# A planner's prices for GpSimd and wide matmuls, and a ring of five split weights instead of four, in a hybrid decoder trunk

## The chip, the cores and the metric

The kernel runs on one core of a Trainium2 chip. The metric is the device time of one execution in microseconds (us). TensorE is PE in the rows, its weight loads PEld, VectorE DVE, ScalarE ACT, GpSimd POOL, and SyncE, which issues the DMAs here, SP. Each engine works through its own instructions in order; semaphores hold an instruction until those of other engines are done.

## The reference

One layer of a decoder trunk for 2048 prompt tokens and 8 requests of 4 tokens with the same weights (width 1024, MLP width 4096), all in fp32:

```python
h = _rmsnorm(x, norm1_g) * (1.0 + sc1) + sh1
proj = h @ w_in                     # 1024 -> 2824 columns
z, xbc, dt, frw, us5 = jnp.split(proj, list(IN_SPLITS), axis=-1)
y_ssd, ... = _ssd_mixer(z, xbc, dt, ...)      # Mamba-2, chunked
y_rw, ...  = _rwkv_mixer(frw, ...)            # RWKV-7, a recurrence
y_s5, ...  = _s5_mixer(us5, ...)              # complex diagonal SSM + GLU
mix = jnp.concatenate([y_ssd, y_rw, y_s5], axis=-1) @ w_out
x = x + g1 * mix
h2 = _rmsnorm(x, norm2_g) * (1.0 + sc2) + sh2
ff = jnp.square(jax.nn.relu(h2 @ mlp_w1)) @ mlp_w2
x = x + g2 * ff
```

A last RMSNorm follows, and the mixers' new states are outputs too.

## The kernel before

**Tiles and stages.** The tokens are four blocks of 512 columns; block 1 also carries the 32 columns of the short requests (544, computed as two pieces of 272). Stage by stage, PE projects the four blocks through `w_in`, then for blocks 0 and 1 computes `w_out` and the MLP, and from about 2050 us on `paired` computes the rest for blocks 2 and 3 together, with fewer products by sums of blocks. The mixers of all blocks run between, as narrow fp32 matmuls and work of DVE, ACT and POOL, and fill in beside the wide matmuls.

**Wide matmuls and split weights.** A wide product is made of fp32r matmuls, 128 x 128 weights by 512 or 272 columns. For accuracy each operand is split into a high and a low part, and three matmuls (high x high, high x low, low x high) make one. A weight tile of 128 x 1024 comes by DMA into one of four raw buffers in `arena` and is used as two halves of 512 columns, 12 matmuls each for 512 columns of tokens. `wprep` has ACT cast a half's high part, and `wlow` has POOL subtract it from the raw half for the low part; both land in one of `NWH` = 4 slots of a ring in `arena_r`. `whalf` (for the projections and the MLP) and `wop` (in `paired`) take the next half and call `wprep` and `wlow` for later ones. `gemm2` starts a projection with two products at once and so holds four halves, all slots of the ring.

**Memory.** `arena_r` holds 14336 columns of split activations, then the ring. `arena_b` (14336) and the part of `arena` behind A_C (A_L columns) hold the mixers' temporaries; a mixer is admitted while the costs of those running are at most ROOM = 18364 columns. A generator that finds no room yields; an evacuation of a wide product (`mal`) waits.

**What sets the order.** The program is written out once, in the order in which instructions are called, with a clock for each engine in `Plan`: every call adds a price (`Eng.__getattr__`) and starts at the latest of its engine's clock and its operands' times. Between matmuls, `pump` steps the generators of the mixers whose operands are ready by PE's clock. So the prices decide behind which wide matmul a narrow one is written, and how far ahead of use a cast is written follows from `wprep` and `wlow`. All engine instructions are called at line 201, so the rows all show L201, and tiles have the names `arena`, `arena_b`, `arena_r`, `arena_t` (it takes the place of `arena_b` in `paired`) and `bk` for the eight PSUM banks.

Of the kernel before, what the change touches and what calls it, by code (L numbers as in the profile page):

```python
# [22 lines left out]
LS = 4  # L23
W = 544
A_T = 14336
A_R = A_T + 5600
NRB = 4
A_C = 7296 + 1024 * NRB
A_L = 11360
A_F = A_C + A_L  # L30
ROOM = 18364
NPLAIN = 2
# [159 lines left out]
class Eng:  # L192
# [3 lines left out]
    def __getattr__(self, op):  # L196
        fn = getattr(self.real, op)
        plan, name = self.plan, self.name

        def call(*a, **k):  # L200
            r = fn(*a, **k)  # L201
            aps = [x for x in list(a) + list(k.values()) if hasattr(x, "tensor")]
            out, ins = aps[:1], aps[1:]
            n = 1
            for c in out[0].shape[1:]:
                n *= c
            dma = 0
            if name == "PE":
                m = out[0].shape[0]
                if "r" in str(ins[0].dtype)[-1]:  # L210
                    cost = max(n / 2.4 + 2.5, 107)
                elif op == "transpose":
                    cost = 110
                elif m > 64:
                    cost = max(n / 0.6, 215)
                elif m > 32:
                    cost = max(n / 0.86, 100)
                else:
                    cost = max(n / 1.4, 68)
            elif name == "DVE":  # L220
                ps = any(x.tensor.name.startswith("bk") for x in aps)
                if op in ("tensor_scalar", "tensor_copy", "memset") and not ps:
                    cost = 65 + 0.53 * n
                elif op == "tensor_reduce":
                    i = 1
                    for c in ins[0].shape[1:]:
                        i *= c
                    cost = 70 + 1.04 * i
                elif op == "tensor_tensor_scan":
                    cost = 70 + 2.1 * n  # L230
                elif op == "reciprocal":
                    cost = 70 + 8.3 * n
                else:
                    cost = 72 + 1.04 * n + (30 if ps else 0)
            elif name == "ACT":
                cost = 95 + 0.833 * n
            elif name == "POOL":
                cost = 60 + (2.4 if op == "tensor_tensor" else 0.9) * n
            else:
                cost = 0  # L240
                dma = 4.0
                for c in out[0].shape:
                    dma *= c
            plan.run(name, cost, out, ins, dma)
            return r

        return call
# [3 lines left out]
def layer_kernel(ctx: ExitStack, tc: tile.TileContext, d, o, dbg=None):  # L251
# [7 lines left out]
    arena = sbp.tile([128, A_F], F32, name="arena")  # L259
    arena_r = sbp.tile([128, A_R], F32R, name="arena_r")  # L260
    swap = [ExitStack()]
# [4 lines left out]
    M = Mem(arena[:, 0:A_C], A_C)  # L266
    M1 = Mem(arena[:, A_C:], A_L)
    MB1 = Mem(arena_b, A_T)
    MT = Mem(arena_r[:, 0:A_T], A_T, True)
    MR = Mem(arena_r[:, A_T:], A_R - A_T, True)  # L270
    A1, AR, AT, AM = [MB1, M1], [MR], [MT], [M, MB1, M1]
# [405 lines left out]
            yield from finish()  # L677


    NWH = 4  # L680
    wring = [(MR.get(512), MR.get(512)) for _ in range(NWH)]
    wbuf = M.get(1024 * NRB)
    wraw = [wbuf.f[:, 1024 * i:1024 * i + 1024] for i in range(NRB)]
# [2 lines left out]
    class WS:  # L686
# [3 lines left out]
        pos = 0  # L690
# [9 lines left out]
    def whalves(i):  # L700
        hi, lo = wring[i % NWH]
        return hi, lo, wraw[i // 2 % NRB][:, 512 * (i % 2):512 * (i % 2) + 512]
# [3 lines left out]
    def wprep(upto):  # L706
        while WS.ready < min(upto, len(wops)):
            i = WS.ready
            wload(wops[i][0] + 1)
            hi, lo = wring[i % NWH]  # L710
            sm = wops[i][1]
            if sm is None:
                act(hi.r, whalves(i)[2])
            else:
                wsrc[i] = sm.get(wops[i][2])
                act(sm.shape(hi.r), wsrc[i])
            WS.ready += 1

    def wlow(upto):
        while WS.low < min(upto, WS.ready):  # L720
            i = WS.low
            hi, lo = wring[i % NWH]
            sm = wops[i][1]
# [18 lines left out]
    def whalf():  # L742
        i = WS.pos
        WS.pos += 1
        wprep(i + 3)
        wlow(i + 1)
        hi, lo = wring[i % NWH]
        return hi.r, lo.r

# [104 lines left out]
    def pieces(hasS):  # L854
        return [(0, 272), (272, 544)] if hasS else [(0, BT)]
# [16 lines left out]
    def gemm(xs, hasS, drop=()):  # L872
        nk = len(xs)
        got, ws = [], []
        for (c0, c1) in pieces(hasS):
            bk = gbank()
            assert bk is not None
            n = c1 - c0
            cnt = 0
            for k in range(nk):  # L880
                if k % 4 == 0 and k // 4 == len(ws):
                    ws.append(whalf())
                if k % 4 == 2:
                    wlow(WS.pos + 2)
                hi, lo = ws[k // 4]
                xh, xl = xs[k]
                h_, l_ = hi[:, 128 * (k % 4):128 * (k % 4) + 128], lo[:, 128 * (k % 4):128 * (k % 4) + 128]
                for i, (w_, x_) in enumerate(((h_, xh), (h_, xl), (l_, xh))):
                    x_ = x_[:, c0:c1]
                    t = plan.when([w_, x_], "PE")  # L890
                    while t > plan.clk["PE"] + 150 and pump(t - plan.clk["PE"]):
                        pass
                    mm(bk[:, 0:n], w_, x_, start=cnt == 0, stop=cnt == nk * 3 - 1)
                    cnt += 1
                    if i == 2 and drop and c1 >= BT:
                        free(*drop[k])
                    if cnt % SLOT == 0 and cnt < nk * 3:
                        pump()
            got.append((bk, c0, c1))
        return got  # L900

    def gemm2(acts, hasS):
        units = [(m, p) for m in range(2) for p in pieces(hasS)]
        nt = 2
        bks = [wait_for(gbank, "bank") for _ in units]
        cnt = 0
        for k in range(8):
            if k > 0 or not WS.pos:
                wait_for(lambda: len(acts) > k, "acts")
            if k == 0:  # L910
                pos = WS.pos
                wprep(pos + 2 * nt)
                wlow(pos + 2 * nt)
                WS.pos += 2 * nt
                wait_for(lambda: len(acts) > k, "acts")
            if k == 6:
                wprep(WS.pos + 1)
                wlow(WS.pos + 1)
            xh, xl = (x.r for x in acts[k])
            for u, (m, (c0, c1)) in enumerate(units):  # L920
                hi, lo = (w.r for w in wring[(pos + 2 * m + k // 4) % NWH])
                h_, l_ = hi[:, 128 * (k % 4):128 * (k % 4) + 128], lo[:, 128 * (k % 4):128 * (k % 4) + 128]
                for i, (w_, x_) in enumerate(((h_, xh), (h_, xl), (l_, xh))):
                    x_ = x_[:, c0:c1]
                    t = plan.when([w_, x_], "PE")
                    while t > plan.clk["PE"] + 150 and pump(t - plan.clk["PE"]):
                        pass
                    mm(bks[u][:, 0:c1 - c0], w_, x_, start=k + i == 0, stop=k == 7 and i == 2)
                    cnt += 1
                    if cnt % SLOT == 0 and cnt < 24 * len(units):  # L930
                        pump()
        wprep(WS.pos + 3)
        for m in range(2):
            yield [(bks[u], c0, c1) for u, (j, (c0, c1)) in enumerate(units) if j == m]

# [1674 lines left out]
    def wop():  # L2610
        i = WS.pos
        WS.pos += 1
        wprep(i + 3)
        wlow(i + 1)
        hi, lo = wring[i % NWH]
        return hi.r, lo.r

    def product(bk, w, col, units, first, k_done=0):
        n = len(units) * 3
        cnt = 0  # L2620
        for k, (xh, xl) in enumerate(units):
            c = col + 128 * k
            for w_, x_ in ((w[0], xh), (w[0], xl), (w[1], xh)):
                w_ = w_[:, c:c + 128]
                t = plan.when([w_, x_], "PE")
                while t > plan.clk["PE"] + 150 and pump(t - plan.clk["PE"]):
                    pass
                T.matmul(bk, w_, x_, start=first and cnt == 0, stop=cnt == n - 1, skip_group_check=True)
                cnt += 1
                if cnt % SLOT == 0 and cnt < n:  # L2630
                    pump()
                if cnt == n // 2:
                    wlow(WS.pos + 1)
        pump()

    def paired(last, ys):
# [555 lines left out]
```

## Time and profile before

| | us |
|---|---|
| median of 3 runs | 2949.0 (2939.87 to 2949.55) |
| the profiled execution | 2948.27 |
| its span, first to last instruction | 2946.5 |
| PE busy | 2709.7 (92%) |
| DVE busy | 1916.1 (65%) |
| POOL busy | 1474.9 (50%) |
| ACT busy | 1099.3 (37%) |
| mean granted clock of TensorE | 0.950 |

A row of windows gives busy time and the count of instructions for each engine in a stretch, and the granted clock (PEclk): 1.00 is 2.4 GHz, 0.50 is 1.2 GHz. A row of waits says which instructions stood idle for which releaser, the total, the number and the longest. A row of the timeline gives the start, the time, the engine, the operation, the tiles (written <- read), the shape and the count of merged instructions, and in brackets the idle time before it and what ended it. Times of matmuls overlap, so a step is read from a long run of equal ones.

### The profile page before, as it was taken

How to read it: one execution, taken by the hardware profiler on the slowest of the kernel's cores; microseconds unless marked ns; L12 is line 12 of the kernel's file. 1: busy time of each engine (PE TensorE's matmuls, PEld its weight loads, DVE VectorE, ACT ScalarE, POOL GpSimd, SP SyncE). 2: the span in 40 equal slices, each digit the busy share in tenths (PEclk: the TensorE clock that was granted, in tenths of full speed). 3: DMA queues.
4: the chain of work that ended last, by engine and by line, in shares of the span. 5: the costliest groups of instructions: out<-in, count | busy, mean ns of one | idle time of the engine just before them, and what ended most of it. 6: DMA issues, size and time to landing. Idle time of an engine off the chain costs nothing.

```text
span 2946.5 us, 44466 instructions
## 1 busy us (share of the span) xinstructions
PE 2709.7 (92%) x16267; PEld 2250.1 (76%) x16267; DVE 1916.1 (65%) x3553; ACT 1099.3 (37%) x2049; POOL 1474.9 (50%) x1274
## 2 busy tenths in 40 slices
PE   7888988999997999999898998999996999989997
PEld 5567876676776777777687898999985778868886
DVE  5885786676675535556776768563354644478777
ACT  5354343444332333433333432333444222344332
POOL 2255344344454434354432444343444877768883
PEclk9898999999998899999998999999998999999998
DMA  8466546545643333345542453422453344374431
GB/s 281 147 208 201 183 159 206 170 140 154 197 122 136 111 117 117 115 146 159 176 142 74 140 192 95 146 92 89 139 190 109 140 150 157 144 274 143 143 136 58
DMA packets 329766, 441.86 MB, mean 150 GB/s; under 512 B 87620, under 2 KB 199364, under 8 KB 329548
## 3 DMA queue, kind: packets, MB, share of 16 engines
q1 hardware_dynamic: 329548, 439.02, 44.7%
q8 instruction: 128, 2.10, 0.3%
q14 instruction: 90, 0.74, 0.1%
HBM read 331.77 MB, written 107.18 MB: 149 GB/s over the span
## 4 chain that ended last, share of the span: by engine, by line
PE 48%; DVE 9%; issue 3%; POOL 1%; DMA 1%; ACT 1%; SPq 0%; DVEq 0%; POOLq 0%; ACTq 0%
PE bk L201 48%; DVE arena_b L201 5%; DVE arena L201 3%; POOL arena_r L201 1%; DVE arena_r L201 1%; ACT arena_b L201 1%; DMA sphid<-arena 0%; DVE arena_t L201 0%; ACT arena_r L201 0%; POOL arena L201 0%; SPq L201 0%; DMA arena_r<-sphid 0%; ACT arena L201 0%; DMA arena_b<-sph 0%; DMA arena_b<-spk 0%
## 5 line engine op out<-in xcount | busy, mean ns | idle before, releaser
L201 PE MATMUL bk<-arena_r 128*128 128x512 f32 (+1 forms) x9376 | 1861.4, 353 | 121.7 <-ACT arena_r L201 51.3
L201 PEld LDWEIGHTS bk<-arena_r 128*128 128x128 f32 x9376 | 1509.1, 193 | 379.5 <-ACT arena_r L201 60.8
L201 POOL TENSOR_TENSOR arena_r<-arena,arena_r 128x512 fp32r<-128x512 f32 (+1 forms) x795 | 1084.8, 1379 | 1051.3 <-ACT arena_r L201 929.0
L201 ACT ACTIVATE arena_r<-arena 128x512 fp32r<-128x512 f32 x757 | 459.8, 626 | 452.0 <-PE bk L201 257.1
L201 ACT ACTIVATE arena_b<-bk 128x512 f32<-128x512 f32 (+10 forms) x478 | 202.1, 446 | 787.2 <-PE bk L201 542.6
L201 PE MATMUL bk<-arena_t,arena_r 128*128 128x512 f32 x1584 | 397.9, 401 | 26.1 <-DVE arena_t L201 12.4
L201 PEld LDWEIGHTS bk<-arena_t,arena_r 128*128 128x128 f32 x1584 | 301.8, 191 | 102.2 <-DVE arena_t L201 14.9
L201 DVE SCALAR_TENSOR_TENSOR arena<-bk,arena 128x512 f32<-128x512 f32 (+1 forms) x370 | 232.5, 641 | 213.0 <-PE bk L201 207.5
L201 DVE TENSOR_TENSOR arena_b<-arena_b 128x256 f32<-128x256 f32 (+19 forms) x481 | 262.3, 555 | 51.4 <-ACT arena_b L201 34.3
L201 POOL TENSOR_TENSOR arena<-arena 128x512 f32<-128x512 f32 (+1 forms) x142 | 208.4, 1467 | 87.3 <-DVE arena L201 81.2
L201 DVE TENSOR_TENSOR arena<-arena,bk 128x512 f32<-128x512 f32 (+2 forms) x189 | 124.6, 669 | 174.4 <-PE bk L201 143.1
L201 PE MATMUL bk<-arena_b 32*32 32x128 f32 (+11 forms) x2424 | 221.4, 273 | 6.2 <-DVE arena L201 3.4
L201 PEld LDWEIGHTS bk<-arena_b 32*32 32x32 f32 (+6 forms) x2424 | 183.4, 149 | 44.9 <-issue 17.7
L201 DVE SCALAR_TENSOR_TENSOR arena_b<-arena_b,arena 128x512 f32<-128x512 f32 (+4 forms) x234 | 141.5, 619 | 36.9 <-POOL arena_b L201 16.7
L201 PE MATMUL bk<-arena,arena_b 128*64 128x128 f32 (+8 forms) x1035 | 138.2, 279 | 25.5 <-DVE arena_b L201 18.7
L201 PE MATMUL bk<-arena 128*64 128x128 f32 (+7 forms) x1214 | 132.2, 322 | 30.9 <-DVE arena L201 16.5
L201 DVE TENSOR_TENSOR arena_r<-arena_b,arena_r 128x512 fp32r<-128x512 f32 (+1 forms) x113 | 90.5, 808 | 100.3 <-ACT arena_r L201 99.5
L201 DVE TENSOR_TENSOR arena<-arena 128x512 f32<-128x512 f32 (+14 forms) x188 | 144.7, 779 | 14.6 <-ACT arena L201 8.6
L201 PEld LDWEIGHTS bk<-arena,arena_b 128*128 128x128 f32 (+4 forms) x1035 | 111.2, 163 | 54.3 <-DVE arena_b L201 21.1
L201 PEld LDWEIGHTS bk<-arena 128*64 128x64 f32 (+4 forms) x1214 | 107.2, 166 | 58.4 <-DVE arena L201 17.6
L201 ACT ACTIVATE arena_b<-arena_b 128x512 f32<-128x512 f32 (+4 forms) x176 | 106.3, 610 | 119.9 <-DVE arena_b L201 99.4
L201 DVE TENSOR_TENSOR arena_b<-arena_b,arena 128x4 f32<-128x4 f32 (+13 forms) x223 | 118.3, 552 | 18.9 <-POOL arena L201 6.6
(79 smaller groups left out, 1664.5 us busy)
## 6 DMA issues: line engine op xcount, KB each, us to landing
arena<-in_w SPq DMA_DIRECT2D x196, 512.0 KB
arena<-in_w_in SPq DMA_DIRECT2D x88, 512.0 KB
sphid<-arena SPq DMA_DIRECT2D x112, 256.0 KB
arena<-in_ada_w SPq DMA_DIRECT2D x16, 1024.0 KB
arena<-in_w_out SPq DMA_DIRECT2D x32, 512.0 KB
arena_t<-sphid SPq DMA_DIRECT2D x30, 512.0 KB
arena_b<-spk SPq DMA_DIRECT2D x29, 512.0 KB
arena_r<-sphid SPq DMA_DIRECT2D x26, 512.0 KB
```

What stands on the lines that cost most here:

```text
L201: r = fn(*a, **k)
```

## The change

Two things. The prices of `Eng.__getattr__` change for fp32r matmuls on PE (from n/2.4 + 2.5 to n/2.36 + 9 ns) and for POOL: copies 150 + 1.1 n instead of 60 + 0.9 n, `tensor_tensor` up to 16 columns (these are powers, for reciprocal roots) 320 + 210 n, wider ones 70 + 2.45 n instead of 60 + 2.4 n. And the ring has five slots; `wprep` and `wlow` are called for one half more ahead at each place. The fifth slot's 1024 columns come out of A_L. The operations and their shapes are the same; with the prices, the order of all engines changes.

```diff
-A_R = A_T + 5600
+A_R = A_T + 6624
-A_L = 11360
+A_L = 10336
                 if "r" in str(ins[0].dtype)[-1]:
-                    cost = max(n / 2.4 + 2.5, 107)
+                    cost = max(n / 2.36 + 9, 107)
             elif name == "POOL":
-                cost = 60 + (2.4 if op == "tensor_tensor" else 0.9) * n
+                if op == "tensor_copy":
+                    cost = 150 + 1.1 * n
+                elif op == "tensor_tensor" and n <= 16:
+                    cost = 320 + 210 * n
+                elif op == "tensor_tensor":
+                    cost = 70 + 2.45 * n
+                else:
+                    cost = 60 + 0.9 * n
...
-    NWH = 4
+    NWH = 5
+    AHEAD = NWH - 3
...
     def whalf():
         i = WS.pos
         WS.pos += 1
-        wprep(i + 3)
-        wlow(i + 1)
+        wprep(i + AHEAD + 2)
+        wlow(i + AHEAD)
...
                 if k % 4 == 2:
-                    wlow(WS.pos + 2)
+                    wlow(WS.pos + AHEAD + 1)
...
                 pos = WS.pos
-                wprep(pos + 2 * nt)
+                wprep(pos + 2 * nt + AHEAD - 1)
                 wlow(pos + 2 * nt)
...
             if k == 6:
-                wprep(WS.pos + 1)
-                wlow(WS.pos + 1)
+                wprep(WS.pos + AHEAD)
+                wlow(WS.pos + AHEAD)
...
-        wprep(WS.pos + 3)
+        wprep(WS.pos + AHEAD + 2)
...
     def wop():
         i = WS.pos
         WS.pos += 1
-        wprep(i + 3)
-        wlow(i + 1)
+        wprep(i + AHEAD + 2)
+        wlow(i + AHEAD)
...
                 if cnt == n // 2:
-                    wlow(WS.pos + 1)
+                    wlow(WS.pos + AHEAD)
```

**ACT at the start of block 1's projection (its pair of products).** `arena_r<-arena 128x512` is the cast of a weight half, `arena_r<-arena_b 128x544` that of an activation of block 1, `arena_b<-bk_70 128x512 x2` the evacuation of block 0's last product, beside which the pair's first matmul is written. Before:

```order
L201 ACTIVATE arena_b<-arena_b,arena 128x512
L201 ACTIVATE arena_r<-arena 128x512
L201 ACTIVATE arena_r<-arena_b 128x544
L201 ACTIVATE arena_b<-arena_b,arena 128x512
L201 ACTIVATE arena_b<-bk_70 128x512 x2
L201 ACTIVATE arena_r<-arena_b 128x544
L201 ACTIVATE arena_r<-arena 128x512 x2
L201 ACTIVATE arena<-bk_76 128x256
```

Now:

```order
L201 ACTIVATE arena_r<-arena 128x512
L201 ACTIVATE arena_r<-arena_b 128x544
L201 ACTIVATE arena_b<-arena_b,arena 128x512
L201 ACTIVATE arena_r<-arena 128x512
L201 ACTIVATE arena_b<-bk_70 128x512 x2
L201 ACTIVATE arena_r<-arena_b 128x544
L201 ACTIVATE arena_b<-arena_b,arena 128x512
L201 ACTIVATE arena_r<-arena_b 128x544
L201 ACTIVATE arena_r<-arena 128x512 x2
L201 ACTIVATE arena_b<-bk_73,arena 128x512
```

The `x2` was the pair's third and fourth half, the third with no matmul left between its cast and its use; now the third is cast ahead of the evacuation, and the `x2` is the fourth and a fifth half, 41 matmuls ahead of the fourth's use.

**ACT later in the same projection, where block 2's input is first read.** `arena_b<-arena_b 128x512` are squares of block 2's `x`, just loaded, and the rows with `bk` around them evacuate products of block 1. Before:

```order
L201 ACTIVATE arena_b<-bk_70 128x8x4
L201 ACTIVATE arena_b<-bk_70,arena 128x32
L201 ACTIVATE arena_b<-arena_b 128x512 x2
L201 ACTIVATE arena_r<-arena 128x512
L201 ACTIVATE arena<-bk_73 128x272
```

Now:

```order
L201 ACTIVATE arena_b<-bk_76 128x8x4
L201 ACTIVATE arena_b<-bk_76,arena 128x32
L201 ACTIVATE arena_b<-arena_b 128x512
L201 ACTIVATE arena<-arena_b 128x512
L201 ACTIVATE arena_r<-arena 128x512
L201 ACTIVATE arena<-bk_70 128x272
```

Nothing moved: two squares (the second now writes to `arena`) still stand directly ahead of the cast of a half, which has 0 matmuls before its first use before and 5 now.

**POOL where the solve of block 0's recurrence begins.** `arena_r<-arena,arena_r 128x512` is the low part of a weight half, the memsets clear the solve's tile, and the copies are of the convolution's edge columns. Before:

```order
L201 COPY arena_b<-arena 128x3
L201 COPY arena<-arena_b 128x3
L201 MEMSET arena_b 64x1024
L201 MEMSET arena_b 64x32
L201 TENSOR_TENSOR arena_r<-arena,arena_r 128x512
L201 COPY arena_b<-arena 128x4 x2
```

Now:

```order
L201 COPY arena<-arena_b 128x24
L201 TENSOR_TENSOR arena_r<-arena,arena_r 128x512
L201 MEMSET arena_b 64x1024
L201 MEMSET arena_b 64x32
L201 TENSOR_TENSOR arena_r<-arena,arena_r 128x512 x2
L201 TENSOR_TENSOR arena<-arena_b,arena 128x1
```

A low part stands ahead of the memsets now, and the first one behind them is used 39 matmuls later instead of at once.

## Rows read from the trace of the kernel before

**Rows 1.** Windows, the first 2250 us: length, busy by engine (instructions), PEclk, DMA share, GB/s.

```profile
0.00:2250.00 2250.00, 2073.24 (x13575) 1738.85 (x13576) 1447.26 (x3015) 862.59 (x1685) 951.32 (x914) 0.95 0.47 152
```

**Rows 2.** Waits of PE in the first 2250 us: total us, times, longest.

```profile
PE bk L201 <- POOL arena_r L201: 41.8, 19, 9.0
PE bk L201 <- ACT arena_r L201: 37.3, 11, 9.5
PE bk L201 <- DVE arena L201: 24.4, 15, 10.6
PE bk L201 <- DVE arena_b L201: 23.2, 13, 13.4
...
PE bk L201 <- POOL arena L201: 6.2, 5, 1.9
```

**Rows 3.** Timeline of PE at its longest waits for `arena_r`.

```profile
222.71 0.82 PE L201 MATMUL bk<-arena_r 128*128 128x272 f32 x2 [7.28 <-ACT arena_r L201]
...
257.29 0.82 PE L201 MATMUL bk<-arena_r 128*128 128x272 f32 x2 [9.54 <-ACT arena_r L201]
...
420.99 1.27 PE L201 MATMUL bk<-arena_r 128*128 128x272 f32 x4 [8.73 <-POOL arena_r L201]
...
473.80 1.22 PE L201 MATMUL bk<-arena_r 128*128 128x512 f32 x2 [8.99 <-POOL arena_r L201]
...
683.29 0.80 PE L201 MATMUL bk<-arena_r 128*128 128x512 f32 x1 [4.03 <-ACT arena_r L201]
...
1471.10 1.27 PE L201 MATMUL bk<-arena_r 128*128 128x272 f32 x4 [5.42 <-POOL arena_r L201]
...
1598.54 0.82 PE L201 MATMUL bk<-arena_r 128*128 128x272 f32 x2 [5.66 <-ACT arena_r L201]
```

**Rows 4.** Timeline of ACT and POOL: what stood ahead of three late weights.

```profile
255.41 1.31 ACT L201 ACTIVATE arena_b<-arena_b 128x512 f32<-128x512 f32 x2 [11.73 <-DMA arena_b<-in_x]
...
418.29 1.15 POOL L201 MEMSET arena_b<- 64x1024 f32 x2 [7.98 <-DMA spl<-arena_b]
...
466.97 1.62 POOL L201 TENSOR_TENSOR arena_b<-arena_b 128x504 f32<-128x504 f32 x1 [5.94 <-DVE arena_b L201]
```

**Rows 5.** Windows, stretches at half clock behind late weights, and the sum of all 15.

```profile
195.10:198.50 3.40, 3.40 (x30) 2.16 (x32) 3.40 (x5) 3.40 (x7) 3.34 (x4) 0.50 0.68 263
219.00:229.20 10.20, 5.83 (x24) 5.51 (x25) 10.03 (x19) 2.49 (x6) 6.23 (x5) 0.50 0.46 154
249.70:263.30 13.60, 6.01 (x18) 4.26 (x19) 2.74 (x4) 5.45 (x13) 5.08 (x7) 0.50 0.85 299
...
416.90:427.20 10.30, 6.21 (x27) 6.21 (x28) 6.86 (x15) 0.69 (x2) 5.92 (x9) 0.50 0.69 194
...
468.10:478.40 10.30, 4.60 (x19) 4.41 (x20) 4.51 (x6) 1.26 (x2) 8.74 (x11) 0.50 0.77 213
...
1468.20:1475.10 6.90, 4.00 (x18) 4.00 (x19) 6.52 (x13) 3.13 (x6) 4.79 (x5) 0.51 0.93 308
1594.50:1604.80 10.30, 5.71 (x23) 5.39 (x24) 9.90 (x20) 6.54 (x11) 4.28 (x3) 0.50 0.15 51
...
sum 95.70, PE 66.26 PEld 57.49 DVE 63.36 ACT 27.25 POOL 59.92; mean PE 4.42 PEld 3.83 DVE 4.22 ACT 1.82 POOL 4.00
```

**Rows 6.** Timeline of PE, long runs of wide matmuls of both widths at 2.4 GHz.

```profile
2718.25 19.22 PE L201 MATMUL bk<-arena_r 128*128 128x512 f32 x84
...
2039.77 20.40 PE L201 MATMUL bk<-arena_r 128*128 128x272 f32 x161
```

**Rows 7.** Lines of POOL by form: count, busy us, mean ns, idle before.

```profile
L201 POOL TENSOR_TENSOR arena_r<-arena,arena_r 128x512 fp32r<-128x512 f32 x791 | 1082.4, 1383 | 1051.3 <-ACT arena_r L201 929.0 <-PE bk L201 69.6 <-ACT arena_b L201 22.7
...
L201 POOL TENSOR_TENSOR arena<-arena_b,arena 128x4 f32<-128x4 f32 x16 | 17.7, 1105 | 42.5 <-DVE arena_b L201 42.2
```

**Rows 8.** Timeline of PE, the longest wait behind 2250 us.

```profile
2267.54 0.79 PE L201 MATMUL bk<-arena_t,arena_r 128*128 128x512 f32 x1 [7.70 <-ACT arena_t L201]
```

**Rows 9.** Lines of DVE by form: additions with one input from PSUM, with both from SBUF.

```profile
L201 DVE TENSOR_TENSOR arena<-arena,bk 128x512 f32<-128x512 f32 x178 | 119.8, 683 | 173.4 <-PE bk L201 142.3 <-ACT arena_r L201 24.7 <-DMA arena<-in_w 4.1
L201 DVE TENSOR_TENSOR arena<-arena 128x512 f32<-128x512 f32 x112 | 112.6, 1017 | 12.4 <-ACT arena L201 8.5 <-POOL arena_t L201 1.5
```

## The prediction

> **What bounds the kernel now.** I read the windows first, for which engine is full and at what clock; then PE's waits; then the timeline at the longest of them; last, the queues that held the late operand. In the first 2250 us PE is busy for 2073.24, DVE for 1447.26, POOL for 951.32 and ACT for 862.59 [rows 1]: PE is the bound, so what counts is PE's idle time and the time that it spends at 1.2 GHz. Up to there only one tile holds both weights and activations, `arena_r`, and the waits on it come to 41.8 (from POOL, which makes the low parts) and 37.3 us (from ACT, which makes the high parts), 79.1 together in 30 waits [rows 2]. Almost all of it is split weights that came late. Seven of the 30 make 49.65 us [rows 3]; the other 23 make 29.5, 1.3 each.
>
> Why they are late is seen on the queue in front of the late operand. At 257.29 PE waits 9.54 us for a cast that stands on ACT behind two squares, and the first of these waited 11.73 us for a load of `x`. At 420.99 and 473.80 the low part stands on POOL behind a memset that waited 7.98 us for a store, and behind a subtraction that waited 5.94 us for DVE [rows 4]. These are queues in order: a wait of the mixers ahead of a split becomes a wait of PE when the split is needed soon after it.
>
> Each such wait costs twice. In 15 stretches (95.7 us), each at or just behind one of them, the granted clock is 0.50, the 1.2 GHz level, after PE had stood idle; PE is busy for 66.26 us in them [rows 5], work that takes half as long at 2.4 GHz: 33.1 us lost. So weights that come late cost 79 + 33 = 112 us of this execution, 3.8%.
>
> **The change part by part.** *Ring of five.* Casts and splits are neither added nor removed; each is written one half earlier. A half is 12 matmuls of 512 columns, at 19.22 us / 84 = 0.229 us, so 2.75 us; in block 1, whose columns go in two pieces of 272, it is 12 matmuls a piece at 20.40 / 161 = 0.127, so 1.5 us [rows 6]. That alone covers nearly all of the 23 short waits, but not the seven long ones, and the order says more than the mean: of 1440 casts and low parts, 45 stand fewer than 12 matmuls ahead of their first use before, and 14 now; the median goes from 35 matmuls to 48. Scaled by these counts, 79.1 x 14/45 = 24.6 us stay and **54.5 go**. The long waits taken one by one agree. At the three starts of a projection pair (7.28, 4.03 and 5.66 us) the third and fourth halves were cast at the pair's own start; now the third is cast before it and the fourth stands 41 matmuls ahead: gone. The wait of 9.54 stays: the order of ACT has the squares ahead of a needed cast as before. Behind the memset the low part now stands 39 matmuls ahead, 39 x 0.127 = 5.0 us, so 8.73 - 5.0 = 3.7 stay. That of 8.99 goes (3 matmuls before, over 30 now). Of 5.42 take off one half, 2.7 stay. That is 16 us, and of the short ones (14 - 3)/(45 - 7) of 29.5 = 8.5: 24.5 in all.
>
> *Clock.* The stretches at 249.70 and 1468.20 stay, that at 416.90 by half: 6.01 + 4.00 + 3.1 = 13 us of busy time; of the rest, 66.26 - 6.0 - 4.0 - 6.2 - 4.6 (that at 468.10) = 45.4, the same 11/38, 13 us. These 26 us at 1.2 GHz still lose 13: **20 of 33 go** [rows 5].
>
> *Given back.* While PE stood, the mixers' chains on DVE ran on. In 8 of the 15 stretches DVE is busy for over 95%, from the one at 195.10 to the one at 1594.50, 41 us together, though it is at 64% in the first 2250 us [rows 1, 5]. With PE no longer standing there, a part of this work becomes what PE waits for. None of it is the lower bound, all 41 us the upper; I take a third, **+14**, because in the other seven stretches DVE has room.
>
> *Prices of wide matmuls.* They go from 215.8 to 226 ns at 512 columns and from 115.8 to 124 at 272; the rows say 229 and 127 [rows 6], so the plan now runs at PE's pace. It also takes away a spare of 4.5%: a narrow matmul put 3 us behind its operand used to get 3.0 x 229/215.8 = 3.18 us and now gets 3.04. Over the 28 waits on DVE's results [rows 2] that is 0.14 x 28 = 4 us at most. The Trainium skill speaks against this price: "TensorE: Matmul & The Clock Gate", section "Wait — 56ns, not 53.3ns?", gives N/2.4 + 2.5 ns from start to start, 215.7 ns at 512 columns, which is the old formula. By it the new price would be too high, narrow matmuls would come too early, and the sum would be some 4 us longer; the trace's 229 ns disagrees with it, and the measurement decides.
>
> *Prices of GpSimd.* The power of a 128x4 tile was planned at 70 ns and takes 1105, now priced 1160; the 128x512 split was 1289, takes 1383 and is now 1324 [rows 7]. Consumers of powers are set a microsecond later. PE's waits on such results are 6.2 us [rows 2], so the gain is 0 to 6; I set it against the 4 us above: 0, with ends of -6 and +4.
>
> *Others, at nothing.* 1024 columns go from the mixers' memory to the ring (rival, below). A pair asks for a fifth cast at its start, 0.6 us on ACT, under PE's first 12 matmuls; uncovered, 0.6 us for each pair, some 5 us. On SP a fourth weight load stands ahead of block 1's first loads of `x`, which nothing waits for so early. From 2250 us on PE's waits are on activations, as the 7.70 us at 2267.54 [rows 8], in chains that the change leaves in place.
>
> **Sum.** The profiled execution took 2948.27 us (span 2946.5), 0.7 below the median of 2949.0, so the sum stands for either: 2948.3 - 54.5 - 20 + 14 = **2888**. Its own bounds: with nothing given back and all of the 112 us gone, 2948 - 112 - 6 = 2830; with all 41 given back, 2948.3 - 74.5 + 41 + 4 + 5 = 2924.
>
> **The rivals.** *DVE takes the place of the late weights.* For it: the 8 full stretches, and mixers that now run denser, with more splits beside DVE's work. A DVE addition with two inputs from SBUF takes 1017 ns where one with an input from PSUM takes 683 [rows 9]. If DVE's and POOL's meetings stretch the 41 us by that ratio, 61 us come back, and the gain is 74.5 - 61 = 13: 2935, within 0.5%. Against it: 64% is no full engine. The Trainium skill has a rule for this, "SBUF — State Buffer", section "Who interferes with whom": DVE instructions with two SBUF inputs and GpSimd's reads exclude each other for a whole instruction; the two means agree with it.
>
> *The shorter memory stalls PE: slower.* The mixers' temporaries have 24672 columns instead of 25696 while admission still counts 18364, so what is left for stores, squares and evacuations falls from 7332 to 6308. Where none is free, the evacuation of a wide product waits and the next one is written only after it. A spot of this kind costs what the stretch at 219.00 shows, 10.2 us with PE busy for 5.83 at half clock: 4.4 + 2.9 = 7.3 us [rows 5]. It decides from 8 to 9 spots on (60.5 / 7.3); 12 give 2888 + 88 = 2976. Against it: the 2,700th of the 2,812 narrow matmuls stands behind 6,716 wide ones before and 6,652 now, so the mixers aren't pushed back.
>
> *The casts are early but blocked all the same.* The slot that a cast waits for is freed at the same matmul as before, so if that were what held ACT and POOL, nothing would change: 2949. Against it: the rows name a load, a store and DVE as what held them [rows 4].
>
> **How the numbers follow.** Forecast (2860 to 2925): 0.66. Nearly all late weights gone (2830 to 2860): 0.06. DVE in their place, 0.12, half of it just over and half within 0.5%. Blocked all the same: 0.07. Memory, slower: 0.09. 0.5%, 15 us, is about what a measurement of this kernel tells from no change. Faster 0.66 + 0.06 + 0.06 = 0.78, within 0.13, slower 0.09. The range of 8 in 10 leaves out the slower case, the blocked one and the lowest: 2850 to 2936.
>
> **What would show it.** PE's waits on `arena_r` up to 2250 us should fall from 79 to some 25, from POOL and from ACT alike, with one of 7 to 10 us left where squares of `x` stand ahead of a cast. With 26 of 66 us of that work left, some 58 us less are spent at 1.2 GHz, and the mean clock of the first 2250 us should rise from 0.95 to 0.96. Waits on DVE's tiles may rise by 14 us. The last 700 us should be the same within a few us. I am wrong if the waits on `arena_r` stay above 50, if waits on DVE grow by more than 40, or if PE waits with narrow work missing where before it had none.

## The result and the profile after

The changed kernel takes **2910.4 us** (median of 4 runs, 2904.6 to 2913.6) where the kernel before takes 2948.6 beside it: a ratio of **0.9875 (95% interval 0.985 to 0.9899)**, 38 us less. The prediction was 2888, with a range of 2850 to 2936: right in direction and inside the range, but 22 us too good. Its profiled execution has a span of 2908.4 us, 38.1 less than before.

The first 2206 us of it hold about as many matmuls as the first 2250 before [rows 1], and end at the same place of the program. The windows of after, in the columns of [rows 1] (PE, PEld, DVE, ACT, POOL, granted clock, DMA share, GB/s), for that part and for the rest:

```profile
0.00:2206.00 2206.00, 2052.99 (x13567) 1726.03 (x13567) 1453.12 (x3014) 862.85 (x1684) 962.38 (x916) 0.96 0.48 155
2206.00:2908.00 702.00, 641.69 (x2700) 516.10 (x2700) 470.32 (x540) 236.01 (x366) 522.57 (x358) 0.95 0.40 143
```

And the rest of the kernel before:

```profile
2250.00:2946.00 696.00, 636.44 (x2694) 511.25 (x2692) 468.88 (x538) 236.68 (x364) 523.57 (x361) 0.95 0.40 144
```

So 44 us are won up to that place and 6 are lost behind it, in `paired`. PE's waits in the first 2206 us of after, to be held against [rows 2]:

```profile
PE bk L201 <- DVE arena_b L201: 50.8, 21, 13.7
PE bk L201 <- DVE arena L201: 19.9, 9, 7.1
PE bk L201 <- ACT arena L201: 17.6, 5, 5.9
PE bk L201 <- ACT arena_r L201: 16.2, 9, 8.0
...
PE bk L201 <- POOL arena_r L201: 4.6, 5, 1.5
```

The waits on `arena_r` from POOL and ACT fell from 79.1 to 20.8 us (some 25 were expected); those on DVE's `arena_b` rose from 23.2 to 50.8. One wait of 8.0 on ACT's `arena_r` is new, and it is not for a weight at all.

**An accounting that closes.** Of every trace I took three sums: PE's waits of over 60 ns; which of them are for a half of split weights (told by the address of the late operand), up to the first matmul of `paired`; and half of PE's busy time in the stretches at 1.2 GHz, since that work takes about half as long at 2.4 (in after, wide matmuls follow each other at 427 ns in the slow stretches and 230 in the others with 512 columns, at 227 and 125 with 272, so what is lost is 45 to 46%, a little under the half). The span less all waits less that half is 2616.5 us before and 2613.8 after. Over the twelve profiled executions that do the whole work it lies between 2608.6 and 2622.5, while their spans go from 2893 to 2955. So a change of order alters the time through these two things and hardly anything else. The sums are of one execution each, which can lie off the median (by 10 us in ring5_late, by 7 in ring6). In us (waits up to `paired`, the half over the whole execution; the last column counts the waits up to `paired`, of either kind, during at least 90% of which DVE was busy):

| kernel | median | ratio | for split weights | other waits | half of work at 1.2 GHz | waits with DVE full |
|---|---|---|---|---|---|---|
| before | 2948.6 | 1 | 76.4 | 98.7 | 105.6 | 93.0 |
| after | 2910.4 | 0.9875 | 10.0 | 140.6 | 93.3 | 88.8 |
| ring5_only | 2898.0 | 0.9839 | 12.0 | 141.1 | 77.3 | 90.1 |
| prices_only | 2957.2 | 1.0036 | 65.7 | 122.0 | 89.1 | 96.3 |
| memory_only | 2923.4 | 0.9929 | 69.0 | 96.9 | 90.6 | 95.4 |
| after_honest | 2905.4 | 0.9858 | 16.1 | 132.7 | 101.2 | 82.9 |
| before_nudge | 2945.6 | 0.9999 | 74.8 | 98.7 | 110.2 | 99.7 |
| ring5_nudge | 2893.6 | 0.9833 | 13.1 | 138.8 | 81.8 | 82.7 |
| ring5_late | 2947.0 | 1.0011 | 60.3 | 108.6 | 121.9 | 88.0 |
| ring6 | 2931.3 | 0.9956 | 3.3 | 155.5 | 114.7 | 97.1 |
| ring5_margin | 2935.6 | 0.9967 | 27.8 | 143.0 | 104.7 | 74.3 |
| ring5_pe | 2925.8 | 0.9924 | 25.8 | 140.3 | 97.2 | 97.5 |
| ring5_lite | 2812.9 | 0.9560 | 10.9 | 89.4 | 64.8 | 36.1 |
| before_lite | 2855.7 | 0.9706 | 56.0 | 72.5 | 82.3 | 62.4 |

The 38 us from before to after are thus -66.4 of waits for split weights, +41.9 of other waits up to `paired`, +1.4 of waits in it, -12.3 at 1.2 GHz and -2.7 of rest. The question for the chip was where the 41.9 come from.

### The profile page after: what moved, and what is told of

Same layout as the page of the kernel before. It is cut to its first block, busy times and chain, and to the rows that moved or that the text cites. A ratio compares the mean times of both kernels' runs of the same rounds, so it can differ in the third digit from the quotient of the medians.

```text
span 2908.4 us, 44455 instructions
## 1 busy us (share of the span) xinstructions
PE 2694.7 (93%) x16267; PEld 2242.1 (77%) x16267; DVE 1923.4 (66%) x3553; ACT 1098.9 (38%) x2049; POOL 1485.0 (51%) x1274
## 5 line engine op out<-in xcount | busy, mean ns | idle before, releaser
L201 POOL TENSOR_TENSOR arena_r<-arena,arena_r 128x512 fp32r<-128x512 f32 x795 | 1105.2, 1404 | 992.7 <-ACT arena_r L201 916.3
L201 ACT ACTIVATE arena_r<-arena 128x512 fp32r<-128x512 f32 (+1 forms) x784 | 473.4, 626 | 418.1 <-PE bk L201 197.6
L201 ACT ACTIVATE arena_b<-bk 128x512 f32<-128x512 f32 (+9 forms) x455 | 193.2, 448 | 765.6 <-PE bk L201 476.8
L201 DVE SCALAR_TENSOR_TENSOR arena<-bk,arena 128x512 f32<-128x512 f32 (+2 forms) x330 | 201.3, 628 | 139.7 <-PE bk L201 139.1
L201 DVE TENSOR_TENSOR arena_b<-arena_b 128x512 f32<-128x512 f32 (+18 forms) x401 | 222.7, 567 | 58.8 <-ACT arena_b L201 41.0
L201 PE MATMUL bk<-arena_b 32*32 32x128 f32 (+10 forms) x1928 | 184.1, 274 | 14.1 <-DVE arena_b L201 9.0
L201 PEld LDWEIGHTS bk<-arena_b 128*128 128x128 f32 (+6 forms) x1928 | 153.0, 153 | 43.8 <-issue 18.2
L201 PE MATMUL bk<-arena,arena_b 128*64 128x128 f32 (+11 forms) x1295 | 143.3, 267 | 41.6 <-DVE arena_b L201 23.1
L201 PE MATMUL bk<-arena 128*64 128x128 f32 (+11 forms) x1212 | 135.9, 319 | 33.7 <-ACT arena L201 17.0
L201 DVE TENSOR_TENSOR arena<-arena 128x512 f32<-128x512 f32 (+13 forms) x208 | 148.6, 725 | 17.4 <-ACT arena L201 10.8
L201 ACT ACTIVATE arena_b<-arena_b 128x512 f32<-128x512 f32 (+6 forms) x168 | 101.0, 608 | 116.1 <-DVE arena_b L201 93.3
```

## The experiments

The theories, as they were named on record: **A**, the earlier casts alone make the gain, and the mixers' lateness, which had lain under PE's standing for weights, comes up as other waits; **B**, the dearer price of wide matmuls takes away the narrow matmuls' spare and brings 33 us of the other waits; **C**, the prices bring the gain; **D**, the shorter memory takes part of it back; and later **L**, every order draws its waits anew, and the other waits of the ring of five are an unlucky draw.

### One part alone

**ring5_only**: the change without its prices.

```diff
-                    cost = max(n / 2.36 + 9, 107)
+                    cost = max(n / 2.4 + 2.5, 107)
...
-                if op == "tensor_copy":
-                    cost = 150 + 1.1 * n
...
+                cost = 60 + (2.4 if op == "tensor_tensor" else 0.9) * n
```

> The ring of five with the old prices. Theory A (the ring alone makes the gain; the 33 us of other waits that came back are what the mixers had done while PE stood for weights): 2895 to 2920, PE's waits on arena_r in the projections and MLPs near 20 us, the other waits there near 130 as in the changed kernel. Theory B (the dearer wide matmul takes spare from the narrow ones and brings the 33 us): the other waits stay near 97 as before, the time is 2865 to 2885. Theory C (the prices make the gain, the ring little): 2935 to 2950.

2898.0 us, ratio 0.9839 (0.9819 to 0.9858): all of the gain and more. Waits for split weights 12.0, other waits 141.1, as in after. The 42 us came with the ring, not with a price: A stands, C falls, B falls as the explanation of after.

**prices_only**: four slots, the new prices.

```diff
-                    cost = max(n / 2.4 + 2.5, 107)
+                    cost = max(n / 2.36 + 9, 107)
...
-                cost = 60 + (2.4 if op == "tensor_tensor" else 0.9) * n
+                if op == "tensor_copy":
+                    cost = 150 + 1.1 * n
...
```

> The new prices with the ring of four. Theory A: the waits on arena_r stay at 70 to 85 us in the first 2250 us, the others near 97, the time within 10 us of before (2940 to 2960). Theory B: the others rise to some 130 us and the time to 2970 to 2985. Theory C: 2905 to 2920.

2957.2 us, 1.0036 (1.002 to 1.0052): 11 us slower. Other waits 122.0, up by 23; those for split weights 65.7. The time is A's; the other waits lie between A's 97 and B's 130, nearer to B's.

**memory_only**: the kernel before with 1024 columns less for the mixers.

```diff
-A_L = 11360
+A_L = 10336
```

> The kernel before with 1024 columns fewer for the mixers and nothing else. Rival D (the shorter memory took back part of the gain): 2960 to 2980. All others: within 10 us of before, 2940 to 2960; what it differs by is also how far a new order alone moves the time.

2923.4 us, 0.9929 (0.9907 to 0.9952): *faster* by 0.7%, though it only takes memory away, and below every range named for it. The waits fell by 9 us together (69.0 and 96.9), half of the work at 1.2 GHz by 15, from 105.6 to 90.6. D falls, and a warning comes with it: an order that is new for no reason can be worth 20 us.

**after_honest**: after, with the planner's prices of DVE and ACT raised nearer to the measured durations.

```diff
-                    cost = 72 + 1.04 * n + (30 if ps else 0)
+                    cost = 85 + 1.24 * n + (0 if ps else 60)
             elif name == "ACT":
-                cost = 95 + 0.833 * n
+                cost = 100 + 1.0 * n
```

> The changed kernel with DVE and ACT priced by the trace as well (512 columns on DVE 720 to 780 ns instead of 604 to 634, on ACT 612 instead of 521). If the waits on DVE and ACT came back because these two engines are still priced too low beside PE, the other waits fall from 130 to some 100 us and the time to 2870 to 2890. If they came back because the chains themselves are that long, the time is 2900 to 2925.

2905.4 us, 0.9858 (0.9841 to 0.9875), other waits 132.7: 8 less than in after. Too low prices for DVE and ACT are not the main cause.

### Is it the draw of an order?

**before_nudge** and **ring5_nudge**: a neutral constant of the planner is moved, in the kernel before and in ring5_only.

```diff
-    BWAIT = 250
+    BWAIT = 260
```

> The kernel before, with one constant of the planner moved: a bank counts as free 260 ns after its last reader instead of 250. Nothing else; the order of the narrow work changes by it. It asks how far an order's time moves for no reason at all. Theory A (the late weights hid the mixers' lateness, the ring alone took them away): 2930 to 2960, PE's waits on split weights 65 to 80 us up to the start of the stage for blocks 2 and 3, all other waits 90 to 115. Theory L (a new order draws its waits anew, and the other waits of the ring of five are only an unlucky draw): a spread as wide as 20 us either way, other waits anywhere from 95 to 140.

> The ring of five with the old prices, and the same constant moved from 250 to 260 ns. Theory A: 2890 to 2915, waits on split weights 8 to 18 us, all other waits again 130 to 145, for a fourth order with five slots. Theory L: the other waits are drawn anew and may fall to 100, which would give some 2860 to 2880.

In the kernel before the constant moved no instruction, so this was the same program once more: 2945.6 us, 0.9999 (0.9983 to 1.0014), the three sums of its trace within 5 us of before's, its waits with DVE full within 7. It says nothing on L, but how far such sums repeat. In ring5_only it did move the order: 2893.6 us, 0.9833 (0.9808 to 0.9858), waits for split weights 13.1, other waits 138.8. With the later runs, seven orders with early casts have other waits of 133 to 156, and the four with casts at the old lead 97 to 122. L falls for the waits, if by little: without the one wait of 8 to 9 us that all seven share (below), theirs are 125 to 147. In time the two groups overlap: the seven have ratios of 0.9833 to 0.9967, the four of 0.9929 to 1.0036. The means, 0.9893 and 0.9994, are 30 us apart, and a single order lies up to some 20 us from the mean of its group.

### Are the extra waits DVE's?

**ring5_lite** and **before_lite**: DVE's multiply-adds in place of 240 columns and more are left out, 540 of its 3553 instructions; the order of PE, ACT and POOL is kept.

```diff
-            r = fn(*a, **k)
...
+            key = [(x.tensor.name, x.offset) for x in aps]
+            fma = op == "scalar_tensor_tensor" and key[0] in key[1:] and str(a[-1]).endswith("add") and n >= 240
+            r = None if fma else fn(*a, **k)
```

> The ring of five with the old prices, every instruction of PE, ACT and POOL in the same order, but DVE's multiply-adds in place of 240 columns and more are left out (the planner still counts them): some 350 instructions, about 210 us of DVE's time before the stage for blocks 2 and 3. Theory A, DVE's lateness is what came up when the late weights went: the 141 us of other waits fall by the extra 42 and more, to 95 or less, close to those of the next run. If the extra waits are not DVE's, but ACT's, POOL's or the loads', they fall by no more than in the next run, and some 40 us of difference between the two stay.

> The kernel before, in its own order, with the same multiply-adds of DVE left out. Theory A: PE stands for split weights anyway, so less DVE work brings little here: waits on split weights 60 to 76, other waits from 98 to some 80 to 90. If the two kernels' difference is not DVE's: other waits fall by as much as in the run before this one.

Other waits fell from 141.1 to 89.4 with five slots and from 98.7 to 72.5 with four: of the 42 us of difference 17 are left. Waits with DVE full fell by 54 and by 31. So most of the extra waits, 25 us of the 42, hang on DVE's work, as A has it. What A did not say: the time falls alike, by the ratios 82 us with five slots and 87 with four, because in the kernel before the waits for split weights fell as well, by 20 us. So the ring itself is worth no more beside a lighter DVE, 43 us against 47: of the waits up to `paired` it takes off more there (28 us net against 22), at 1.2 GHz it wins less (17.5 against 28.3). PE's waits in the first 2140 us of before_lite (its helper is line 208):

```profile
PE bk L208 <- ACT arena_r L208: 34.1, 10, 9.7
PE bk L208 <- DVE arena_b L208: 26.1, 10, 14.0
PE bk L208 <- POOL arena_r L208: 24.8, 14, 9.0
```

POOL's `arena_r`, 41.8 in [rows 2], is down to 24.8, while ACT's is 34.1, near its 37.3. The late low parts were partly DVE's lateness too, passed on through POOL's queue, as [rows 4] shows for one of them.

### The cast's place or the fifth slot?

**ring5_late**: five slots, but casts and low parts are called no earlier than before.

```diff
-    AHEAD = NWH - 3
+    AHEAD = 1
```

> Five slots and the old prices, but casts and low parts are called no earlier than in the kernel before: 38 of 1440 stand fewer than 12 matmuls ahead of their first use (45 before, 23 with the ring of five alone). It asks which half of the ring's edit did it. If a cast's place in its queue decides, as the prediction has it: waits on split weights 55 to 70 of the 76 before, time 2915 to 2945, with what the smaller memory brings in it. If the slot's release held the casts: the fifth slot alone takes the waits to 20 or less, other waits rise to 130 or more, and the time is 2890 to 2905.

2947.0 us, 1.0011 (0.9994 to 1.0028): no gain at all, 2 us above the range for the cast's place; waits for split weights 60.3, within it. Four of the seven waits of [rows 3] are back at the same places of the program (counted in wide matmuls), in the timeline of PE:

```profile
224.43 0.82 PE L201 MATMUL bk<-arena_r 128*128 128x272 f32 x2 [7.13 <-ACT arena_r L201]
...
259.75 0.82 PE L201 MATMUL bk<-arena_r 128*128 128x272 f32 x2 [10.41 <-ACT arena_r L201]
...
424.83 18.92 PE L201 MATMUL bk<-arena_r 128*128 128x272 f32 x133 [7.01 <-POOL arena_r L201]
...
477.51 1.22 PE L201 MATMUL bk<-arena_r 128*128 128x512 f32 x2 [8.59 <-POOL arena_r L201]
```

7.13, 10.41, 7.01 and 8.59 here, 7.28, 9.54, 8.73 and 8.99 in [rows 3]. The fifth slot by itself wins nothing; the place of the cast in ACT's and POOL's queues is what decides.

### More of it

**ring6**: six slots, one half more ahead.

```diff
-A_R = A_T + 6624
+A_R = A_T + 7648
-A_L = 10336
+A_L = 9312
-    NWH = 5
+    NWH = 6
```

> Six slots, one half more ahead again, old prices, 1024 columns less for the mixers' temporaries. 6 of 1440 casts and low parts stand fewer than 12 matmuls ahead, so waits on split weights should be 2 to 8 us (12 with five slots). Theory A (what PE stands for now is the mixers' lateness): other waits stay at 135 to 150 and the time is within 10 us of the ring of five, 2888 to 2908. If the other waits grow with every slot because casts written early stand in front of the mixers' work on ACT and POOL: 155 or more, 2905 to 2920.

2931.3 us, 0.9956 (0.9943 to 0.9969): 33 us slower than five slots. Waits for split weights are down to 3.3, other waits up to 155.5; both sums together went from 153 to 159, which is 6 us. The rest is the clock: 106 waits instead of 84, and 37 us more lost at 1.2 GHz. A fails here: 155.5 is above its 135 to 150 and just in the 155 or more of the other theory, and the time is above the ranges of both, which left the clock out. Whether early casts now stand in the mixers' way, this run does not tell.

**ring5_margin**: ring5_only, with narrow matmuls at the earliest 1200 ns behind the planned end of their operands.

```diff
-    MRANK, MARGIN = 0.05, 600
+    MRANK, MARGIN = 0.05, 1200
```

> The ring of five with the old prices, and a narrow matmul is written at the earliest 1200 ns behind the planned end of its operands instead of 600. If the other waits come from too little planned distance: they fall from 141 to 90 to 120 and the time to 2850 to 2885. If they come from chains that run late by several us, through queues, half a microsecond changes little: 125 to 145, 2885 to 2910; and if the mixers are then pushed back behind the wide work, the wait shows at the end of the stage and the time is 2910 or more.

2935.6 us, 0.9967 (0.9951 to 0.9984), other waits 143.0: twice the distance took nothing off them. So they are not short misses of a plan; that the operands are late by whole chains fits, but is not shown by this run. The time is above the range that goes with such waits, and not by a wait at the end of a stage: against ring5_only it lost 15.8 us to waits for split weights, which rose to 27.8 (one of 9.16), and 27.4 at 1.2 GHz.

### The price of wide matmuls

**ring5_pe**: ring5_only with the new price of wide matmuls, GpSimd's prices old.

```diff
-                    cost = max(n / 2.4 + 2.5, 107)
+                    cost = max(n / 2.36 + 9, 107)
```

> The ring of five and the new price of wide matmuls; GpSimd's prices stay old. Both prices together cost 11 to 12 us, with four slots and with five. If the wide price takes away the narrow matmuls' spare: 2905 to 2912 here, with more waits on DVE's tiles than the 64 us of the ring of five alone. If GpSimd's new prices set the narrow work otherwise: 2892 to 2901, as with the ring alone. If it is only another order: waits in sum within 8 us of the 153 of the ring of five alone, and the time anywhere from 2890 to 2935, by the PE work that falls into stretches at 1.2 GHz (118 us there, 198 us with six slots).

2925.8 us, 0.9924 (0.9909 to 0.9938): 28 us slower than ring5_only, above both ranges that rest on a mechanism. The third, only another order, has the time, but its waits should be within 8 us of 153 and are 166. It is not the spare: waits on DVE's `arena` and `arena_b` fell, from 64.5 to 42.5 us (with `arena_r`, from 78.9 to 61.7). Waits for split weights rose from 12.0 to 25.8, and the largest, 7.90 us, is this, in the timeline of PE and of ACT:

```profile
479.66 2.58 PE L201 MATMUL bk<-arena_r 128*128 128x512 f32 x4 [7.90 <-ACT arena_r L201]
```

```profile
477.82 0.63 ACT L201 ACTIVATE arena_b<-arena 128x512 f32<-128x512 f32 x1 [14.16 <-DMA arena<-in_x]
478.46 0.63 ACT L201 ACTIVATE arena<-arena 128x512 f32<-128x512 f32 x1
479.00 0.61 ACT L201 ACTIVATE arena_r<-arena 128x512 fp32r<-128x512 f32 x1
```

ACT stood 14.16 us for a load of `x`, with a needed cast two places behind: the mechanism of the first of [rows 4], at another place. prices_only has such accidents too, with waits of 16.67 us for a cast and, in `paired`, of 12.42 for a low part. In three pairs new prices went the slow way (prices_only against before, after against ring5_only, ring5_pe against ring5_only); in the fourth, GpSimd's prices added to the wide one (after against ring5_pe), they went 15 us the fast way. What the traces show are single accidents of this kind and the clock; whether the prices cost something or three orders were drawn badly stays open.

## Why the prediction was right, and what was 22 us off

The cause was forecast rightly, and the waits for split weights nearly in size. That the time lies within 22 us of the forecast is in part luck: orders with five slots and early casts went from 2893.6 to 2935.6 us.

| term | predicted | measured |
|---|---|---|
| waits for split weights | -54.5 | -66.4 |
| clock | -20 | -18.5 up to `paired`, +6.2 in it |
| given back | +14 | +41.9 |
| last 700 us, waits | 0 | +1.4 |
| rest | 0 | -2.7 |
| sum | -60.5 | -38.1 |

**Ring of five: right in mechanism, a little short.** The prediction sized the waits by the place of casts in their queues, and ring5_late shows that this is the cause: with the fifth slot and the old places 60.3 us of them are there, against 12.0 in ring5_only. It kept 24.6 us, of which 10.0 are there. All seven long waits are gone; the longest left is 2.28 us. The one that was to stay, 9.54 at 257.29, went too: ACT's squares of `x` no longer stand there behind a late load. ACT's waits on loads of `x` in the first 600 us of after:

```profile
ACT arena_b L201 <- DMA arena_b<-in_x: 4.9, 4, 3.2
```

The longest was 11.73 [rows 4] and is 3.2. That was luck of the order, and not a rule: ring5_pe has the same accident with 14.16 us, and over the seven orders with early casts the waits for split weights go from 3 to 28 us, 24.6 among them.

**Clock: right up to `paired`, as a net sum.** PE's busy time at 1.2 GHz up to `paired` fell from 177.5 to 140.5 us, which is 18.5 won of 20 predicted, and the mean of the first part rose from 0.95 to 0.96; the time spent at 1.2 GHz in that part fell from 225 to 181 us, by 44 where some 58 were forecast. New waits brought new slow stretches, which the prediction did not have, and in `paired` the slow work rose from 33.7 to 46.1 us: over the whole execution 12.3 were won. With the steps above, the 66.26 us of slow work in [rows 5] had lost some 30 us rather than 33.1.

**Given back: the step that failed.** The prediction saw that in 8 of the 15 stretches DVE was busy for over 95% [rows 5], 41 us, and took a third of it, "because in the other seven stretches DVE has room". That reason speaks of the other stretches and not of these. Of the 76.4 us of waits for split weights, DVE was full in 36.8 and not full in 39.6. In after the first kind is down to 5.1 and the second to 4.8; and other waits with DVE full rose from 56.2 to 83.7, **by 27.5**. So 31.7 us of waits with DVE full went, and 27.5 came under another name. The size hangs on the line at 90%: at 80% it is 31.8 and 23.2, at 95% 22.4 and 14.6, and without a line, as the time in which PE waits and DVE works, 46.3 and 29.2. By each of these counts some six to nine tenths came back, where the prediction took a third of its 41 us. The sum of all waits with DVE full is 93.0 before and 88.8 after, and between 74 and 100 in all twelve orders (before_nudge, the same program as before, has 99.7). What was won are mostly the waits in which DVE was *not* full: of those for split weights 34.8 went, and 14.4 of others came. Windows of after, four of the waits on narrow operands, taken from those with DVE full (the columns as above):

```profile
110.05:118.39 8.34, 0.00 (x1) 0.00 (x0) 8.13 (x15) 1.91 (x4) 4.06 (x5) 0.76 0.13 37
905.47:912.60 7.13, 0.01 (x1) 0.00 (x0) 6.92 (x15) 1.89 (x4) 1.44 (x1) 0.80 0.00 0
236.00:240.80 4.80, 0.00 (x0) 0.00 (x0) 4.55 (x10) 2.57 (x6) 1.31 (x2) 0.99 0.00 0
393.50:397.00 3.50, 0.17 (x2) 0.00 (x0) 3.33 (x5) 0.54 (x1) 3.11 (x8) 1.00 0.47 188
```

PE does next to nothing in 23.8 us, and DVE works for 22.9 of them, with an engine that is at 66% over the whole part. The pair of kernels with less work on DVE is the test of this reading. From before to ring5_only, waits for split weights with DVE full fall by 28.4 us and other waits with DVE full rise by 25.5; from before_lite to ring5_lite the first fall by 22.3 and the second fall too, by 4.0. With DVE lighter they do not come back; with DVE as loaded as here, most of them did. Waits on DVE's results as a whole rose from 58.9 to 80.4 us, by 21.5 where 14 were forecast, under the 40 at which the prediction called itself wrong.

**The fifth cast, put at nothing: also failed, 8 us and more.** The prediction had a pair of products ask for a fifth cast at its start, 0.6 us on ACT, under PE's first matmuls. At the first pair the cast's weights have not come yet. PE and ACT in the timeline of after:

```profile
32.82 2.89 PE L201 MATMUL bk<-arena 128*32 128x256 f32 x20 [0.36 <-DMA arena<-in_ada_w]
43.72 1.52 PE L201 MATMUL bk<-arena_r 128*128 128x512 f32 x2 [8.01 <-ACT arena_r L201]
45.17 2.89 PE L201 MATMUL bk<-arena 128*32 128x256 f32 x20
```

```profile
27.46 2.38 ACT L201 ACTIVATE arena_r<-arena 128x512 fp32r<-128x512 f32 x4 [0.23 <-DMA arena<-in_w_in]
41.41 0.63 ACT L201 ACTIVATE arena_r<-arena 128x512 fp32r<-128x512 f32 x1 [11.57 <-DMA arena<-in_w_in]
41.94 0.36 ACT L201 ACTIVATE arena<-bk 128x256 f32<-128x256 f32 x1
42.21 0.80 ACT L201 ACTIVATE arena_b<-arena_b,arena 128x512 f32<-128x512 f32 x1
43.04 0.63 ACT L201 ACTIVATE arena_r<-arena_b 128x512 fp32r<-128x512 f32 x1
```

Four casts go at once; the fifth waits 11.57 us for `in_w_in`, and behind it stands the split of an activation (43.04) for which PE waits 8.01. The Trainium skill, "Perfetto Trace Analysis", section "Tensor Engine Instruction (MATMUL, LD_WEIGHTS)", calls ACT, DVE and GpSimd strictly first in, first out; for ACT the trace agrees, with these 11.57 us. The windows from 27 us on, of after and then of before:

```profile
27.00:44.00 17.00, 6.31 (x39) 3.29 (x31) 2.43 (x4) 5.03 (x10) 6.24 (x5) 0.66 1.06 396
44.00:56.50 12.50, 12.50 (x57) 7.63 (x58) 3.35 (x10) 6.21 (x10) 0.00 (x0) 0.51 0.25 100
```

```profile
27.00:44.00 17.00, 14.78 (x94) 8.54 (x90) 5.03 (x13) 9.48 (x17) 4.96 (x4) 0.70 1.06 395
44.00:54.00 10.00, 10.00 (x47) 8.13 (x46) 7.14 (x21) 7.91 (x15) 4.26 (x6) 1.00 0.36 140
```

The DMA engines are full up to 44 us in both, so this load could come sooner only in another's place. PE then works 12.5 us at 0.51, 6 of them lost. In all, PE's 257th matmul, the 81st wide one in both kernels, starts at 58.39 us before and at 71.18 after, 12.8 later. All eight kernels with early casts have this wait, 8.0 to 9.1 us; the six with casts at the old lead do not. So of the 41.9 us of other waits, 8.0 are this cast's, 27.5 by the line at 90% came with DVE full, and the last 6.4 are not explained. A version of ring5_only that asks for the fifth half only once its weights are in was not tried.

**Prices: put at 0 with ends of -6 and +4; all four pairs lie beyond.** With four slots +11 us, with five +12 (after against ring5_only, whose intervals overlap a little), the wide price alone +28, GpSimd's on top of it -15. The argument of the lost spare, 0.14 us each in 28 waits, is not what showed, since DVE's waits fell in ring5_pe. The step treated a price as a shift of single matmuls, but a new price writes a new order, and orders differ by far more than its ends, by what happens to stand in front of a cast and by the clock. What the prices cost by themselves stays open.

**The rivals.** "DVE takes the place of the late weights" was half right: its 61 us came out as 27.5, and not by stretching, since DVE's busy time in the first part went only from 1447.26 to 1453.12 us. "The shorter memory": memory_only shows no such loss. "Early but blocked all the same" asked whether the slot held the casts; ring5_late answers that it did not. The last 700 us were put at no change; 6 us were lost there.

The best version measured is ring5_only, or its nudged order: 0.9833 to 0.9839, by the ratios some 11 to 12 us below the changed kernel, with intervals that overlap a little.

## What to carry to other kernels

Before counting a stall as won, look at what the other engines do while it lasts: a wait of the bound engine in which the next-busiest engine is full is not idle time; here most of it came back under another name. What was won were mostly stalls in which that engine had room. And when work is written earlier in an in-order queue, ask at every place, the first one above all, whether its own input is there: work that comes too early blocks what stands behind it just as late work does.

## What the runs showed of the chip that I had not expected

- The granted clock can make more difference between orders than the waits: ring5_only and ring6 differ by 8 us in all waits of the execution (200.1 and 208.4) and by 37 us in what the work at 1.2 GHz loses.
- An order changed for no purpose moved the time by 20 us (memory_only), while the same program in another call came within 0.01% (before_nudge, by the ratio). An effect of 12 us, as that of the prices, can't be told from the draw by one order of each kind.
- The span is a constant of some 2615 us plus PE's waits plus half of its work at 1.2 GHz, to within 8 us over twelve executions.
